# Gated differential attention on one core: the gate moved between the halves of a head's projection, and two kinds of DMA moved to other queues

## The chip, the cores and the metric

The kernel runs on 1 core of a Trainium2 chip. A core has TensorE (PE, matrix products into PSUM), VectorE (DVE), ScalarE (ACT), GpSimd (POOL) and SyncE (SP, which here only issues DMAs). DMAs are issued from the queues of SyncE, ScalarE or GpSimd and carried out beside the engines. The metric is the device time of one execution in microseconds (us): the median over runs, beside one profiled execution.

## The reference, cut to what matters

One layer of gated differential attention over 1024 tokens of width 1024, with 16 heads:

```python
h = rms_norm(x, norm_g)
q, k, v, z = jnp.split(h @ w_in, 4, axis=-1)          # each 1024 x 2048
q = rms_norm(q.reshape(b, s, 16, 2, 64), q_norm_g) * 64 ** -0.5
k = rms_norm(k.reshape(b, s, 16, 2, 64), k_norm_g)
v = v.reshape(b, s, 16, 128)
# causal, in blocks of 128 queries, with an ALiBi bias:
probs = softmax(einsum('bqhmd,bkhmd->bhmqk', qb, kb) + bias)
weights = probs[:, :, 0] - lam * probs[:, :, 1]
o = einsum('bhqk,bkhe->bqhe', weights, vb)
o = rms_norm(o, head_norm_g) * (1.0 - lam_0)
return x + (o.reshape(b, s, 2048) * jax.nn.silu(z)) @ w_out
```

## The kernel before

**Precision.** A float32 product is made of three float16 products (high by high, high by low, low by high), so each projection piece has three matmul lines: L370 to L372 for q, k, v and L447 to L449 for the gate z. `split_w` turns the raw weights of a head (`raww`, one buffer) into the high and low parts `wsp`: four `Square` passes for a scale (L160), a small matmul, four scalings (L199), and the low parts on VectorE (L205) or GpSimd (L202, L203).

**Heads and rounds.** Heads run in the order `heads`: the odd ones, then the even ones. In a round, `merge` interleaves two generators in proportion to their estimated costs: `attend` of the previous head (eight steps of scores, softmax and transposes, step i on (i+1)*128 keys, and the products with the values) and `project` of the present head. `project` of a head computes q, k and v in two halves of 512 tokens, `for c in range(2)`. A half has four pieces of 128 tokens, each in one PSUM tile `pg`. Each is read out by two ScalarE copies (L422, L423) and one VectorE instruction (L424). `norm(c)` then normalizes q and k of the half, transposes them by DMA (L393) and copies k (L396). After both halves come the two gates, one per 512 tokens: `gate(st, wt, 3, c)` accumulates 24 matmuls in one PSUM tile `pz` and reads it out by a chain that alternates ScalarE and VectorE: Exp (L452), min (L453), Ln (L454), max (L455), Exp (L456), product (L457). The last three heads (`LATE`: 10, 12, 14) project no gate; their three gates follow in `late_gates`.

**PSUM.** `pg`, `pz` and the output tiles share the three banks of the pool `ps_g`. The matmuls of a tile can't start before the tile that had the bank has been read out to its end: for a `pg` that is L424, for a `pz` it is L457.

**Buffers and queues.** The gate's result `sz` has 3 buffers. `finalize` multiplies the head's output with it on GpSimd (L537) and stores the product to DRAM (`g_dram`, L538); a buffer is free when its store has landed. SyncE's queue carries, in the order in which the scheduler put them, the loads of the next head's weights (L136, eight of 256 KB), the transposes of the weights p (L589) and of q and k (L393), the copies of k, and these stores. `prepare` takes one step of the next head's `split_w`; it is called at the end of each q, k, v piece and at every second step of a gate.

**What sets the order.** Each engine runs its instructions in one fixed order. The framework's scheduler sets it when the program is built, from the order of the code, buffers and its own estimates. DMAs of SyncE and ScalarE share eight completion semaphores (`DMAHW0` to `DMAHW7`), so a DMA also waits for the one that used its semaphore before.

## Time and profile before

| | us |
|---|---|
| median of 3 runs (1173.62 to 1181.43) | 1176.65 |
| the profiled execution | 1173.53 |
| its span, first to last instruction | 1171.8 |
| TensorE busy | 1109.9 |
| VectorE busy | 883.0 |
| ScalarE busy | 774.2 |
| GpSimd busy | 272.2 |

The profile's page lists busy time by engine, busy shares in 40 slices, the chain of work that ended last, and groups of instructions by line. Other views of the same trace list instructions in order of time, waits, and busy time by stretch. A matmul's busy time overlaps with its neighbours', so what TensorE could gain is read from its idle time and from start to start. In a row, "L370 PE MATMUL pg<-wsp,h" is line 370, an instruction that writes tile pg from wsp and h; "[2.27 <-DVE sz L457]" means that the engine sat idle for 2.27 us until VectorE's L457 had ended.

### The profile page before, as it was taken

The numbers are of one execution on the slowest core, as the hardware profiler recorded it, in microseconds if no ns is written. First come the engines' busy times: TensorE is split into PE (matmuls) and PEld (weight loads), VectorE is DVE, ScalarE is ACT, GpSimd is POOL, SyncE is SP. The second block draws the span as 40 slices with busy tenths as digits, with TensorE's granted clock in tenths as the row PEclk, the third lists the DMA queues.
The fourth block names the chain that finished last, engine by engine and source line by source line (L and its number), as shares of the span: only waits on it lengthen the run. The fifth ranks groups of instructions, "written<-read, shape, count | busy, mean of one in ns | idle before, by whom it ended". The sixth has DMA issues, their size and how long they took to land.

```text
span 1171.8 us, 18439 instructions
## 1 busy us (share of the span) xinstructions
PE 1109.9 (95%) x6154; PEld 668.5 (57%) x6154; DVE 883.0 (75%) x2180; ACT 774.2 (66%) x1713; POOL 272.2 (23%) x208
## 2 busy tenths in 40 slices
PE   4999999999999999999999999999899997999998
PEld 3555554545555555555545455555455534788887
DVE  6867869787978797879787878788888898563121
ACT  4757778787878797869686978787778776230000
POOL 2220314141314131314131313312121302031000
PEclk7999999999999999999999999999999988999999
DMA  7453736464646464646463645464564457685342
GB/s 222 109 119 52 164 67 140 89 140 85 139 90 137 88 143 89 146 80 133 93 144 76 140 93 126 93 129 100 105 137 87 109 125 182 143 292 179 112 130 70
DMA packets 327887, 143.50 MB, mean 122 GB/s; under 512 B 225136, under 2 KB 307312, under 8 KB 327792
## 3 DMA queue, kind: packets, MB, share of 16 engines
q1 hardware_dynamic: 323040, 133.93, 50.9%
q10 hardware_dynamic: 4752, 8.39, 2.7%
q8 instruction: 48, 0.79, 0.3%
q14 instruction: 47, 0.39, 0.1%
HBM read 63.11 MB, written 16.25 MB: 68 GB/s over the span
## 4 chain that ended last, share of the span: by engine, by line
PE 51%; DVE 20%; ACT 10%; issue 8%; DMA 6%; POOL 2%; SPq 2%; DVEq 0%; ACTq 0%; POOLq 0%
PE pg L370 8%; PE pg L371 8%; PE pg L372 8%; DVE p L559 6%; PE pf L498 5%; PE pf L499 5%; PE pf L500 5%; PE pss L570 3%; DMA raww<-in_l_w_in_dram 3%; DVE p L584 2%; ACT p L576 2%; ACT wsp L160 2%; ACT wsp L199 2%; DMA wt<-p 2%; PE po L601 2%
## 5 line engine op out<-in xcount | busy, mean ns | idle before, releaser
L370 PE MATMUL pg<-wsp,h 128*128 128x384 f16 x1024 | 336.3, 328 | 21.0 <-DVE sz L457 11.9
L372 PE MATMUL pg<-wsp,h 128*128 128x384 f16 x1024 | 336.4, 329 | 1.1 <-DVE h L278 1.1
L371 PE MATMUL pg<-wsp,h 128*128 128x384 f16 x1024 | 336.3, 328 | 1.2 <-POOL wsp L203 1.2
L576 ACT ACTIVATE p<-p,mn 128x128 f32<-128x128 f32 (+7 forms) x256 | 196.4, 768 | 61.0 <-DVE mn L559 59.8
L559 DVE CUSTOM_DVE_ANT_0 p<-pss,toep,nsl 128x512 f32<-128x512 f32 (+3 forms) x256 | 161.2, 642 | 36.8 <-DMA wt<-p 24.6
L570 PE MATMUL pss<-qk 128*128 128x512 f16 (+3 forms) x768 | 164.6, 327 | 11.6 <-DVE mn L559 11.5
L371 PEld LDWEIGHTS <-h 128*128 128x128 f16 x1024 | 100.7, 98 | 86.7 <-issue 26.5
L372 PEld LDWEIGHTS <-h 128*128 128x128 f16 x1024 | 100.6, 98 | 68.2 <-issue 3.7
L66 ACT ACTIVATE p<-p,rc 128x128 f16<-128x128 f32 (+7 forms) x128 | 98.6, 771 | 61.8 <-DVE p L584 60.7
L370 PEld LDWEIGHTS <-h 128*128 128x128 f16 x1024 | 100.7, 98 | 66.6 <-issue 4.1
L584 DVE SCALAR_TENSOR_TENSOR p<-p,rc,p 128x128 f32<-128x128 f32 (+7 forms) x128 | 116.9, 914 | 1.5
L587 DVE SCALAR_TENSOR_TENSOR p<-p,rc,p 128x128 f16<-128x128 f32 (+7 forms) x128 | 104.7, 820 | 14.8 <-ACT p L66 14.6
L570 PEld LDWEIGHTS <-qk 128*128 128x128 f16 x768 | 71.0, 98 | 72.2 <-issue 18.6
L447 PE MATMUL pz<-h,wsp 128*128 128x512 f16 x256 | 98.3, 384 | 1.3 <-DVE sz L457 1.3
L448 PE MATMUL pz<-h,wsp 128*128 128x512 f16 x256 | 98.3, 384 | 0.0
L614 POOL TENSOR_TENSOR sql<-sqo,sqh 128x512 fp32r<-128x512 f32 x30 | 41.7, 1390 | 243.3 <-ACT sqh L612 243.3
L449 PE MATMUL pz<-h,wsp 128*128 128x512 f16 x256 | 98.1, 383 | 0.0
L537 POOL TENSOR_TENSOR sz<-sqo,sz 128x512 f32<-128x512 f32 x26 | 37.7, 1448 | 184.4 <-DVE sqo L631 150.0
L202 POOL TENSOR_SCALAR raww<-raww,scw 128x1024 f32<-128x1024 f32 (+1 forms) x31 | 42.3, 1371 | 159.1 <-ACT wsp L199 127.9
L559 DVE CUSTOM_DVE_ANT_0 p<-pss,toep,mn 128x128 f32<-128x128 f32 (+3 forms) x128 | 75.6, 601 | 0.0
L160 ACT ACTIVATE wsp<-raww 128x1024 f16<-128x1024 f32 x61 | 63.6, 1044 | 14.7 <-DMA raww<-in_l_w_in_dram 9.4
L503 DVE TENSOR_TENSOR xr<-pf,xr 128x512 f32<-128x512 f32 (+1 forms) x33 | 22.1, 671 | 63.4 <-PE pf L500 62.5
(160 smaller groups left out, 2082.9 us busy)
## 6 DMA issues: line engine op xcount, KB each, us to landing
raww<-in_l_w_in_dram SPq DMA_DIRECT2D x96, 256.0 KB, 3.8
rawo<-in_l_w_out_dram SPq DMA_DIRECT2D x32, 256.0 KB, 4.5
qk<-qk SPq DMA_DIRECT2D x64, 128.0 KB, 2.4
raww<-in_l_w_in_dram SPq DMA_DIRECT2D x40, 192.0 KB, 3.7
g_dram<-sz SPq DMA_DIRECT2D x30, 256.0 KB, 2.3
rawg<-g_dram ACTq DMA_DIRECT2D x24, 256.0 KB, 3.5
xt<-in_x_dram SPq DMA_DIRECT2D x8, 512.0 KB, 5.3
xr<-in_x_dram SPq DMA_DIRECT2D x16, 256.0 KB, 3.5
```

Of the source, the lines that this page charges most:

```text
L66: A.activation(out, in_, AF.Copy, scale=scale)
L370: T.matmul(pg, a_h, w_h, start=k == 0, stop=False)
L371: T.matmul(pg, a_h, w_l, start=False, stop=False)
L372: T.matmul(pg, a_l, w_h, start=False, stop=k == KT - 1)
L447: T.matmul(pz, wt["hi"][:, k, n], hh[c][:, k], start=k == 0, stop=False)
L448: T.matmul(pz, wt["hi"][:, k, n], hl[c][:, k], start=False, stop=False)
L449: T.matmul(pz, wt["lo"][:, k, n], hh[c][:, k], start=False, stop=k == KT - 1)
L559: V.tensor_tensor_reduce(out=pm[m][:, o:o + w], in0=pss[:, :w], in1=toep[:, u:u + w], scale=nslope, scalar=3e38 if prev[m] is None else pr ...
L570: T.matmul(pss[m][:, :w].rearrange("p (t q) -> p t q", q=P), qk[:, c, 0, i % 4, m], qk[:, b, v, :w // P, m], start=v == 1, stop=v == 2)
L576: A.activation(pm[m][:, :n], pm[m][:, :n], AF.Exp, scale=-1.0, bias=prev[m], accum_out=sx[:, 1 - m:2 - m])
L584: V.scalar_tensor_tensor(out=p0, in0=p1, scalar=rc[:, 0:1], in1=p0, op0=ALU.mult, op1=ALU.add)
L587: V.scalar_tensor_tensor(out=pl[:, n:], in0=p0, scalar=rc[:, 1:2], in1=pl[:, :n], op0=ALU.mult, op1=ALU.subtract)
```

## The change

The gates of a head are projected between its two halves of q, k, v instead of after them, except in the first head, which keeps its order. `prepare` is called after every half piece in the first half, at every second gate step as before, and at the end of each piece in the second half. The loads of `w_in` are issued from ScalarE's queue, except the first head's; those of a head are put behind the reading of the first piece of the second half (`marks`) of the head two before it. The stores of gated heads are issued from GpSimd's queue. `sz` gets a fourth buffer, and the tile `sqo` of the attention shares the two buffers of `sqk` instead of having its own. Lines behind L136 are numbered 2 to 10 higher in the changed kernel.

```diff
--- before.py
+++ after.py
@@ -133,7 +133,7 @@
             for k in range(KT):
                 rows = wq_view[k * P:(k + 1) * P]
                 bs = slice(blocks[0], blocks[-1] + 1)
-                ins = Q.dma_start(raw[:, k, bs], rows[:, 3, hd] if isinstance(hd, slice) else rows[:, bs, hd])
+                ins = (Q if hd == heads[0] else A).dma_start(raw[:, k, bs], rows[:, 3, hd] if isinstance(hd, slice) else rows[:, bs, hd])
                 if hd == heads[0]:
                     tc.keep_in_program_order(ins)
             return raw, blocks
@@ -351,6 +351,8 @@
         tmp = pool(main, "tmp", bufs=1, reuse_waits="tile")
         sm = pool(main, "sm", bufs=3, reuse_waits="tile")
 
+        marks = []
+
         def project(hd, wt, st):
 
             qk = qkp.tile([P, 2, 3, 4, 2, P], F16, name="qk", tag="qk")
@@ -400,7 +402,10 @@
                 prep.append(split_w(raw0, range(3, 4), wt, hd))
             if nx is not None:
                 st["wt"] = {}
-                prep.append(split_w(*load_raw(nx), st["wt"], nx))
+
+                with tc.issue_after(marks[-1].ins) if marks else ExitStack():
+                    loaded = load_raw(nx)
+                prep.append(split_w(*loaded, st["wt"], nx))
 
             def prepare(pb):
 
@@ -411,7 +416,7 @@
                         return
                     prep.pop(0)
 
-            for c in range(2):
+            def qkv(c):
                 rw = tmp.tile([P, 2, 4, P], F32, name="rw", tag="rw", bufs=2)
                 for t in range(4):
                     pb = ps_g.tile([P, 512], F32, name="pg", tag="pg")
@@ -419,24 +424,29 @@
                     for hf in range(2):
                         gemm_piece(pg, c, t * P, range(hf * 4, hf * 4 + 4))
                         if hf:
-                            A.activation(rw[:, :, t], pg[:, :256].rearrange("p (s b) -> p s b", s=2), AF.Copy)
+                            ev = A.activation(rw[:, :, t], pg[:, :256].rearrange("p (s b) -> p s b", s=2), AF.Copy)
                             A.activation(vh[:, c * 4 + t], pg[:, 256:], AF.Copy, scale=vsc)
                             V.scalar_tensor_tensor(out=vl[:, c * 4 + t], in0=pg[:, 256:], scalar=vsc,
                                                    in1=vh[:, c * 4 + t], op0=ALU.mult, op1=ALU.subtract)
-                            prepare(lambda: pb[:, 384:])
-                        elif hd == heads[0]:
+                            if c or hd != heads[0] or len(prep) > 1:
+                                prepare(lambda: pb[:, 384:])
+                            if t == 0 and c == 1:
+                                marks.append(ev)
+                        elif c == 0 and hd != heads[0] or hd == heads[0] and len(prep) > 1:
                             prepare(None)
                         yield 2.1
                 norm(c, rw)
-            if hd in LATE:
-                while prep:
-                    prepare(None)
-                return
-            for c in range(2):
-                for k in gate(st, wt, 3, c):
-                    if k % 2:
-                        prepare(None)
-                    yield 0.69
+            yield from qkv(0)
+            if hd == heads[0]:
+                yield from qkv(1)
+            if hd not in LATE:
+                for c in range(2):
+                    for k in gate(st, wt, 3, c):
+                        if k % 2:
+                            prepare(None)
+                        yield 0.69
+            if hd != heads[0]:
+                yield from qkv(1)
             while prep:
                 prepare(None)
 
@@ -448,7 +458,7 @@
                 T.matmul(pz, wt["hi"][:, k, n], hl[c][:, k], start=False, stop=False)
                 T.matmul(pz, wt["lo"][:, k, n], hh[c][:, k], start=False, stop=k == KT - 1)
                 yield k
-            e = vp.tile([P, 512], F32, name="sz", tag="sz", bufs=3)
+            e = vp.tile([P, 512], F32, name="sz", tag="sz", bufs=4)
             A.activation(e, pz, AF.Exp, scale=wt["inv"][:, 1, n:n + 1])
             V.tensor_scalar(e, e, 1e18, None, ALU.min)
             A.activation(e, e, AF.Ln, bias=1.0)
@@ -535,7 +545,7 @@
                 return
             e = V if hd in LATE else G
             e.tensor_tensor(z, t1, z, ALU.mult)
-            Q.dma_start(g_dram[c][:, :, place[hd], :].rearrange("t p e -> p t e"), z.rearrange("p (t e) -> p t e", t=4))
+            G.dma_start(g_dram[c][:, :, place[hd], :].rearrange("t p e -> p t e"), z.rearrange("p (t e) -> p t e", t=4))
 
         def attend(hd, st):
 
@@ -605,7 +615,7 @@
                         yield 6 * (4 - il) * P / 2400
                 os = tmp.tile([P, 512], F32, name="os", tag="os")
                 A.activation(os, po, AF.Copy, scale=st["unit"])
-                sq = tmp.tile([P, 512], F32, name="sqo", tag="sqo")
+                sq = tmp.tile([P, 1024], F32, name="sqo", tag="sqk", bufs=2)[:, :512]
                 A.activation(sq, os, AF.Square)
                 sqh = tmp.tile([P, 512], F32R, name="sqh", tag="sqh")
                 e = V if hd == heads[-1] else G
```

On TensorE, before: the end of the fourth head's second gate (`pz_2854`) and the start of the fifth head's first q, k, v piece (`pg_2926`); the score matmuls (`pss`) between them are those of the attention.

```order
L570 LDWEIGHTS qk_2246
L570 MATMUL pss_2902<-qk_2246 128x128
L370 LDWEIGHTS h0_83
L370 MATMUL pg_2926<-wsp_2311,h0_83 128x384
L371 LDWEIGHTS h0_83
L371 MATMUL pg_2926<-wsp_2311,h0_83 128x384
```

In the change the fourth head's second gate (`pz_2585`) is followed by a piece of the same head's second half (`pg_2663`, tokens from `h1`):

```order
L459 LDWEIGHTS wsp_1609
L459 MATMUL pz_2585<-h1_84,wsp_1609 128x512
L372 LDWEIGHTS h1_84
L372 MATMUL pg_2663<-wsp_1609,h1_84 128x384
L373 LDWEIGHTS h1_84
L373 MATMUL pg_2663<-wsp_1609,h1_84 128x384
```

So a gate's bank is now asked for by the second half of its own head, and before by the next head.

On ScalarE, before: from the next head's `Square` passes (L160) to the Exp of the fifth head's second gate (L452, the last row). The names behind "waits" are semaphores: `DMAHW` of DMAs, `Pool`, `DVE` and `PE` of engines.

```order
L160 ACTIVATE wsp,bd<-raww 128x8x128 [waits DMAHW3_49,DMAHW4_49,DMAHW2_49,DMAHW5_49,DMAHW1_49,DMAHW6_49,DMAHW0_49,PE_49]
L391 ACTIVATE sqk<-rw 128x16x64 [waits DVE_49]
L160 ACTIVATE wsp,bd<-raww 128x8x128 x3
L576 ACTIVATE p_3563,sums_458<-p_3563,mn 128x128 [waits DVE_49]
L66 ACTIVATE p_3487<-p_3486,rc 128x1024 [waits DVE_49]
L576 ACTIVATE p_3564,sums_458<-p_3564,mn 128x128 [waits DMAHW7_49,DVE_49]
L422 ACTIVATE rw<-pg 128x2x128 [waits PE_49]
L423 ACTIVATE vh<-pg 128x128
L576 ACTIVATE p_3614,sums_459<-p_3614,mn 128x256 [waits DVE_49,Activation_49]
L576 ACTIVATE p_3615,sums_459<-p_3615,mn 128x256 [waits DMAHW1_49,DVE_49]
L578 ACTIVATE sums_458<-sums_458,nlam 128x1 [waits Activation_49]
L452 ACTIVATE sz<-pz,inv 128x512 [waits DMAHW2_49,Pool_49]
```

In the change, the same gate's Exp is L462; `L136 DMA` are the loads, L617 to L622 read out a product with the values, and L586 and L66 belong to the softmax.

```order
L136 DMA raww<-in_l_w_in_dram 128x4x128
L393 ACTIVATE sqk<-rw 128x16x64 [waits DVE_49]
L617 ACTIVATE os<-po,un 128x512 [waits PE_49]
L136 DMA raww<-in_l_w_in_dram 128x4x128 [waits DMAHW2_49]
L136 DMA raww<-in_l_w_in_dram 128x4x128 [waits DMAHW3_49]
L136 DMA raww<-in_l_w_in_dram 128x4x128
L66 ACTIVATE p_3287<-p_3286,rc 128x768 [waits DVE_49,Activation_49]
L619 ACTIVATE sqo<-os 128x512 [waits Activation_49,Pool_49]
L622 ACTIVATE sqh<-os 128x512
L136 DMA raww<-in_l_w_in_dram 128x4x128 [waits DMAHW5_49]
L462 ACTIVATE sz<-pz,inv 128x512 [waits DMASW5_49]
L136 DMA raww<-in_l_w_in_dram 128x4x128 [waits DMAHW6_49]
```

The Exp stood behind the next head's `Square` passes and the reading of its first piece (L422); it now stands among the loads of the next head's weights, ahead of these passes, and waits for a DMA of GpSimd's queue (`DMASW`).

On SyncE, before, one head's stretch: transposes of p and q/k, loads, a store.

```order
L589 DMA_TRANSPOSE wt_6568<-p_6567 128x10x128
L136 DMA raww<-in_l_w_in_dram 128x4x128 x4
L589 DMA_TRANSPOSE wt_6568<-p_6616 128x12x128
L136 DMA raww<-in_l_w_in_dram 128x4x128 x4
L589 DMA_TRANSPOSE wt_6568<-p_6727 128x14x128
L393 DMA_TRANSPOSE qk<-sqk 128x16x128
L538 DMA g_dram_61<-sz 128x4x128
L396 DMA qk<-qk 64x1024 x2
L589 DMA_TRANSPOSE wt_6568<-p_6813 128x16x128
```

In the change, and below it GpSimd's queue over one head and a bit, with the stores (L548):

```order
L599 DMA_TRANSPOSE wt_5887<-p_5886 128x10x128
L395 DMA_TRANSPOSE qk<-sqk 128x16x128
L599 DMA_TRANSPOSE wt_5887<-p_5947 128x12x128
L398 DMA qk<-qk 64x1024 x2
L599 DMA_TRANSPOSE wt_5887<-p_6061 128x14x128
L599 DMA_TRANSPOSE wt_5887<-p_6129 128x16x128
L599 DMA_TRANSPOSE wt_6226<-p_6225 128x2x128
L599 DMA_TRANSPOSE wt_6226<-p_6280 128x4x128
```

```order
L202 TENSOR_SCALAR raww<-raww,scw 128x8x128 x2
L203 TENSOR_TENSOR wsp<-raww,wsp 128x8x128 x2
L624 TENSOR_TENSOR sql<-sqo,sqh 128x512
L387 TENSOR_TENSOR rw<-rw,gain 128x512
L547 TENSOR_TENSOR sz<-sqo,sz 128x512
L548 DMA g_dram_62<-sz 128x4x128
L624 TENSOR_TENSOR sql<-sqo,sqh 128x512
L547 TENSOR_TENSOR sz<-sqo,sz 128x512
L548 DMA g_dram_61<-sz 128x4x128
```

SyncE keeps the transposes and the copies of k; a store stands directly behind the product (L547) that it stores.

## Rows read from the trace of the kernel before

**Rows 1.** Page, part 1: busy us, share of the span, instructions of each engine.
```profile
PE 1109.9 (95%) x6154; PEld 668.5 (57%) x6154; DVE 883.0 (75%) x2180; ACT 774.2 (66%) x1713; POOL 272.2 (23%) x208
```

**Rows 2.** Busy us by stretch: length, PE, PEld, DVE, ACT, POOL, PEclk, DMA, GB/s.
```profile
22.30:79.80 57.50, 52.71 (x302) 32.28 (x302) 44.23 (x125) 37.88 (x86) 21.34 (x15) 0.92 0.42 114
...
135.20:191.40 56.20, 56.20 (x333) 31.60 (x330) 44.85 (x118) 41.21 (x97) 16.07 (x11) 1.00 0.52 121
...
250.70:309.40 58.70, 56.43 (x333) 31.65 (x331) 48.32 (x122) 46.59 (x105) 15.99 (x10) 1.00 0.55 114
...
871.90:1005.00 133.10, 118.29 (x598) 64.93 (x597) 116.60 (x274) 98.77 (x209) 25.26 (x20) 0.95 0.58 132
```

**Rows 3.** What TensorE waited for, 60 to 820 us: total us, times, longest.
```profile
PE pg L370 <- DVE sz L457: 11.9, 8, 2.3
PE pg L370 <- DVE vl L424: 5.1, 5, 1.6
PE pss L570 <- DVE mn L559: 2.2, 3, 1.4
```

**Rows 4.** TensorE in order of time (start, us, [wait]) up to 258.12 us.
```profile
230.85 0.38 PE L601 MATMUL po<-wt,vh 128*128 128x512 f16 x1
231.06 0.38 PE L602 MATMUL po<-wt,vl 128*128 128x512 f16 x1
...
243.72 0.38 PE L449 MATMUL pz<-h,wsp 128*128 128x512 f16 x1
...
250.25 0.38 PE L449 MATMUL pz<-h,wsp 128*128 128x512 f16 x1
...
250.69 0.33 PE L370 MATMUL pg<-wsp,h 128*128 128x384 f16 x1
...
255.03 0.81 PE L570 MATMUL pss<-qk 128*128 128x384 f16 x4
258.12 0.32 PE L370 MATMUL pg<-wsp,h 128*128 128x384 f16 x1 [2.27 <-DVE sz L457]
```

**Rows 5.** ScalarE in order of time, same stretch: either gate's first Exp.
```profile
246.47 0.67 ACT L452 ACTIVATE sz<-pz,inv 128x512 f32<-128x512 f32 x1
...
264.06 0.69 ACT L452 ACTIVATE sz<-pz,inv 128x512 f32<-128x512 f32 x1 [1.20 <-DMA g_dram<-sz]
```

**Rows 6.** VectorE in order of time: the last step of either gate.
```profile
257.32 0.74 DVE L457 SCALAR_TENSOR_TENSOR sz<-pz,inv,sz 128x512 f32<-128x512 f32 x1
...
269.43 0.74 DVE L457 SCALAR_TENSOR_TENSOR sz<-pz,inv,sz 128x512 f32<-128x512 f32 x1
```

**Rows 7.** DMA issues on SyncE and ScalarE by line: duration ns min/median/max.
```profile
L136 SPq DMA_DIRECT2D raww<-in_l_w_in_dram x144: 327/621/2015, 1.2 to 875.1; - x144
L484 ACTq DMA_DIRECT2D rawg<-g_dram x32: 326/326/477, 904.8 to 1142.3; - x32
L538 SPq DMA_DIRECT2D g_dram<-sz x30: 364/383/1147, 122.1 to 991.9; - x30
```

**Rows 8.** SyncE in order of time: loads between two transposes.
```profile
358.41 2.62 SPq L136 DMA_DIRECT2D raww<-in_l_w_in_dram  x4
362.48 1.45 SPq L589 DMA_TRANSPOSE wt<-p  x1
```

**Rows 9.** What ScalarE waited for up to 820 us: the gate buffer.
```profile
ACT sz L452 <- DMA g_dram<-sz: 2.6, 3, 1.2
```

**Rows 10.** GpSimd's TENSOR_TENSOR of one size: duration ns min/median/max.
```profile
L614 POOL TENSOR_TENSOR sql<-sqo,sqh x30: 1267/1274/1998, 111.2 to 976.9; 128x512 fp32r<-128x512 f32 x30
```

**Rows 11.** SyncE in order of time: the loads for the second and third head.
```profile
41.60 5.40 SPq L136 DMA_DIRECT2D raww<-in_l_w_in_dram  x8
...
73.43 6.93 SPq L136 DMA_DIRECT2D raww<-in_l_w_in_dram  x8
```

**Rows 12.** Busy time by stretch around a fall of the granted clock (PEclk).
```profile
600.00:620.00 20.00, 17.88 (x102) 10.17 (x101) 15.70 (x40) 18.06 (x47) 2.19 (x1) 0.91 0.71 147
```

**Rows 13.** What TensorE waited for from 820 to 1000 us.
```profile
PE pss L570 <- DVE mn L559: 9.2, 9, 2.5
```

## What the change does to the time

> **What bounds the kernel now.** I read the page's busy shares first. TensorE is busy 1109.9 us of 1171.8, VectorE 883.0, ScalarE 774.2, GpSimd 272.2 [rows 1]: nothing but TensorE is near its limit over the whole. Then the busy time by stretch, one stretch for each head [rows 2]. The reader is to see three kinds of stretch there. In the round from 135.2 us TensorE is busy 56.20 of 56.20: that is the floor of a round. A usual round, from 250.7, has 56.43 busy of 58.70, so 2.3 us idle, while VectorE (48.3) and ScalarE (46.6) have some 10 us to spare. In the last rounds, 871.9 to 1005, VectorE has 116.6 of 133.1, and TensorE waits for it. The output after 1005 isn't touched.
>
> Next, what TensorE waited for between 60 and 820 us [rows 3]. Two rows make nearly all of it, both at a `pg` (L370) that wants a PSUM bank: 11.9 us for the gate's product L457 and 5.1 us for L424, the reading of an earlier `pg`. Together they are 17.0 us, plus 2.2 us of scores that wait for the maximum (L559).
>
> The views in order of time show how one arises. The first gate's last matmul ends at 243.72 + 0.38 = 244.10, the second's at 250.63; then comes a piece of the next head, and the following piece could start at 255.03 + 0.81 = 255.84 but starts at 258.12, after 2.27 us for L457 [rows 4]. So TensorE has 255.84 - 244.10 = 11.7 us of other work before it wants the first gate's bank again. The chain that frees it runs from 244.10 over the Exp at 246.47 [rows 5] to the product's end at 257.32 + 0.74 = 258.06 [rows 6]: 14.0 us. The second gate's chain is longer still: its Exp starts only at 264.06 and its product ends at 270.17, 19.5 us after its matmuls. Its bank is out for so long that the next pieces rotate on two banks, which is the L424 row.
>
> **The change part by part.** *Gates between the halves.* No work is added; 24 matmuls of a gate are the same wherever they stand. What counts is TensorE's work between a gate and the next use of its bank. In the changed order 24 gate matmuls, a piece, six instead of four score matmuls of 512 columns, and twelve of an attention output (three each of 512, 384, 256 and 128 columns) stand there; four score matmuls of 384 columns are gone. A matmul of 512 columns starts 231.06 - 230.85 = 0.21 us after the one before it [rows 4]. By columns that is +0.42 for the scores, -0.63 for those gone and 3 x 1280 / 512 x 0.21 = +1.6 for the output: 11.7 becomes 13.1 us. The gates also stand in the attention's middle steps, on 512 to 768 keys and not on 896 and 1024, so the softmax work that its chain queues behind is shorter; my estimate is a chain of 9 to 12 us in place of 14.0. Both move the right way, so I take most of the 11.9 us away. The second gate is another matter: its Exp (now L462) still stands late in ScalarE's order, behind the reading of a piece, an output and six loads. Its bank stays out, and pieces still rotate on two banks. By the same count of columns the time that TensorE gives them rises from about 5 to 6 to 7 us, so I take some of the 5.1 us away too. Together 14 of the 17.0 us; of the 2.2 us for the maximum 1 us, since SyncE brings the transposed weights sooner (next part). That is **-15**. Bounds: -5 if only the first gate's wait halves, -21 if all 19.2 us go and with them the last idle time.
>
> *Loads on ScalarE's queue.* Eight of them a head leave SyncE, where one takes 0.327 to 2.015 us to issue, median 0.621 [rows 7], and where four stand as a block of 2.62 us ahead of a transpose [rows 8]. On ScalarE the nearest row is its own issue of other loads, 0.326 to 0.477 us [rows 7]. So 8 x 0.33 to 8 x 0.62 = 2.6 to 5.0 us a head, and ScalarE has 46.6 of 58.7 us filled [rows 2]: hidden over the round. If that cover were gone it would be 2.6 to 5 us for each of some 12 heads. What is queued behind a load is what stands there in the order: readings of pieces, softmax, the gate's Exp. For the wait on semaphores I take nothing, as the transfers named are old by then.
>
> At the start it isn't hidden. There, the loads of the third head stand on ScalarE in one block ahead of the readings of the second head's pieces, and wait for GpSimd to free `raww`. SyncE took 5.40 and 6.93 us for eight of them there [rows 11]; at ScalarE's 0.326 it would be 2.6. TensorE can lose nothing (if it has pieces left to do) up to 8 us (a block of 6.93 and a reading). I take **+2**, near ScalarE's own row.
>
> *Stores on GpSimd's queue.* SyncE gives away an issue of 0.383 us [rows 7], twice a head. No row shows a DMA of GpSimd. From below it costs nothing: GpSimd is busy 23% [rows 1], and with a fourth `sz` buffer a store has a gate more of time, so that the 2.6 us which ScalarE waited for stores [rows 9] should go. From above: 26 stores at SyncE's 0.383 are +10 if each comes on the path. GpSimd's own instructions are stretched at times, one of 1.267 us to 1.998 [rows 10]. I take **0**, because nothing waits behind the store on GpSimd for long.
>
> A rule of the Trainium skill speaks against this part. "SBUF — State Buffer", section "SBUF: two separate sides", says that a DMA from GpSimd's queue needs descriptors that GpSimd writes through a port shared with VectorE, and that VectorE can lock it out for as long as an instruction runs; it advises the other two queues. By it the stores land late, which is R2 below with its time. The stretch in [rows 10] fits a shared port, and no run here shows it for a store.
>
> *Late part and the clock.* From 871.9 on VectorE's 116.6 us of work is unchanged, and the scores wait for it, 9.2 us from 820 to 1000 [rows 13]. Sooner transposes could give up to -5 there, loads in bursts on ScalarE cost up to +6; I take **0**. A stretch at half clock is seen at 600 to 620, where the mean granted clock is 0.91 [rows 12]; it lies in a round with idle time. Whether it goes is in the bounds (1.6 us at most).
>
> *The sum* is -15 + 2 + 0 + 0 = -13. The profiled execution has 1173.5 us and becomes 1160.5; the median of the three runs is 3.1 above it, so for a median I say 1163.
>
> **The rivals.** *R1, the waits move to the second half.* Between the readings of its first and second piece ScalarE has about 6.9 us of work and eight loads, 9.5 to 11.8 us; TensorE has about 6 to 7 us of work before it wants a bank that is read there. If the reading of a piece is late by 3 us, and the rotation on two banks hides half, 1.5 us a head come back, 11 x 1.5 = 16 us. That takes the gain: 1173.5 - 13 + 16 = 1176, and 1166 to 1181 by how much is hidden. For it speaks that [rows 5] shows the Exp held by ScalarE's order and not by TensorE; against it that the softmax work there is shorter.
>
> *R2, slower: a store comes late.* The second gate's Exp waits for a store from GpSimd's queue, and behind it on ScalarE stand the readings of all further pieces. Before, this wait was 1.20 us once and 2.6 in all [rows 5, 9]. If GpSimd issues or lands a store so late that ScalarE stands 5 us or more at that Exp, TensorE has no more than 1.5 to 2 us left to hide it, and loses 3 us in each of 12 heads: -13 + 36 = +23, about 1197. It decides against the change from about 2 us of TensorE time a head (24 - 13 = +11). For it speaks that the store stands directly behind a product on GpSimd, which has splits of the weights ahead; against it the fourth buffer.
>
> *R3, nothing changes.* The second gate's Exp is as late as before and the first gate's gain is swallowed by the block of loads at the start and by the clock: -15 + 8 + 4 gives about 1171 to 1174.
>
> **How the numbers follow.** My forecast has 0.53, R1 0.22, R2 0.12, R3 0.13. The forecast's own range is 1152 (-21 and -3 late) to 1171 (-5 and +3). About 1% is what a measurement of this kernel can tell from no change: below 1164.9 or above 1188.4. Of the forecast 0.46 lies below 1164.9 and 0.07 above it; R1 and R3 lie within, and of R2 0.10 lies above 1188.4, with 0.02 of R1. So faster 0.46, same 0.42, slower 0.12. The range that leaves out 2 in 10 runs from 1150 to 1182.
>
> **What would show it.** Right: in the view of waits the row of L370's successor (L372) on the gate's product falls from 11.9 to under 3 us, that on the reading of a piece (L424, now L429) doesn't grow; a usual round takes 57 us. R1: the row on the reading grows by what the gate's row loses. R2: ScalarE shows a wait of several us at L462 for a DMA from `sz`, and TensorE's waits stand just behind it. The start is wrong if the second round loses more than 8 us. The stores: GpSimd's issue rows much over 0.8 us. What would make the prediction wrong as a whole is a longer span in rounds with less TensorE idle time, by the clock, which I can't see ahead of the run.

## The result: 1192.22 us, slower by 1.4%

The changed kernel takes 1192.22 us (median of 4 runs, 1190.80 to 1196.35), the kernel before beside it 1175.13. The ratio is 1.0142, 95% interval 1.0093 to 1.0192. 1163 was forecast, with 1150 to 1182 as the range over all rivals. The profiled execution has a span of 1189.0 us, 17.2 more than before's.

Page, part 1 of the changed kernel; [rows 1] is the same line before:

```profile
PE 1115.9 (94%) x6154; PEld 671.3 (56%) x6154; DVE 907.9 (76%) x2180; ACT 770.1 (65%) x1713; POOL 295.5 (25%) x238
```

TensorE is busy 6.0 us longer, though it does the same matmuls; the other 11.2 of the 17.2 us are idle time. Busy time by stretch tells where. First the changed kernel (length, PE, PEld, DVE, ACT, POOL, PEclk, DMA, GB/s, as in [rows 2]): the rounds of the first three heads, a usual one, the ten rounds of the fourth to thirteenth head, and all behind them:

```profile
22.60:84.40 61.80, 55.81 (x312) 33.24 (x312) 45.40 (x132) 37.23 (x86) 14.76 (x11) 0.90 0.34 91
84.40:146.60 62.20, 54.21 (x289) 29.20 (x289) 52.32 (x112) 42.71 (x95) 23.11 (x12) 0.92 0.44 92
146.60:217.30 70.70, 60.62 (x335) 32.75 (x333) 49.99 (x118) 45.02 (x99) 16.19 (x11) 0.95 0.57 108
275.80:334.30 58.50, 56.62 (x333) 31.58 (x331) 50.14 (x123) 45.37 (x103) 16.43 (x13) 1.00 0.55 113
217.30:801.40 584.10, 565.59 (x3295) 315.57 (x3293) 499.20 (x1220) 452.77 (x1018) 167.48 (x124) 1.00 0.57 112
801.40:1189.00 387.60, 370.75 (x1892) 252.18 (x1889) 247.89 (x559) 183.84 (x402) 73.05 (x72) 0.99 0.54 139
```

The kernel before in the stretches that [rows 2] doesn't have, its second round first:

```profile
79.80:135.20 55.40, 53.59 (x308) 29.87 (x306) 44.55 (x116) 41.34 (x93) 11.75 (x7) 0.97 0.50 89
191.40:776.70 585.30, 567.20 (x3293) 316.59 (x3291) 487.53 (x1226) 461.47 (x1022) 154.74 (x102) 1.00 0.55 113
776.70:1171.80 395.10, 372.87 (x1893) 251.52 (x1890) 248.71 (x558) 183.76 (x401) 67.35 (x64) 0.98 0.54 137
```

So the fourth head starts at 217.3 us in place of 191.4: **25.9 us are lost in the first three rounds.** The next ten rounds take 584.1 us in place of 585.3, and all behind them 387.6 in place of 395.1. 25.9 - 1.2 - 7.5 = 17.2. Round by round the first three take 4.3, 6.8 and 14.5 us more than before's. Of their loss 17.5 us are idle time (24.1 us idle in 194.7, before 6.6 in 169.1), and 8.1 us are longer busy time for nearly the same matmuls: the mean granted clock is 0.90, 0.92 and 0.95, before 0.92, 0.97 and 1.00.

What TensorE waited for in the ten rounds, then in the first three, in the changed kernel (us, times, longest):

```profile
PE po L611 <- DMA wt<-p: 8.4, 8, 2.1
PE pss L580 <- DMA qk<-qk: 6.9, 6, 2.5
PE po L611 <- issue: 3.2, 4, 0.9
```

```profile
PE pmn L631 <- POOL sql L624: 4.7, 1, 4.7
PE pg L373 <- POOL wsp L203: 4.5, 2, 3.2
...
PE pss L580 <- DVE mn L569: 3.1, 2, 1.9
...
PE po L611 <- DMA wt<-p: 3.0, 1, 3.0
PE po L611 <- ACT sz L462: 2.9, 1, 2.9
```

The two rows of [rows 3] that the forecast spoke of, 11.9 and 5.1 us, are gone, as forecast. In their place stand 8.4 us for the transposed weights, 6.9 us for the copies of k and 3.2 us of issue (waits of the same matmuls L611 for which the profile shows no releaser), 18.5 together, none of which the prediction had.

**The wait for the copies of k, step by step.** The changed kernel in the fourth head's round, in order of time: loads on ScalarE's queue, VectorE's L394 (the last step of the first half's norm), SyncE's transpose of that half's q and k, its copies, and the first scores of the same head on TensorE.

```profile
257.73 0.55 ACTq L136 DMA_DIRECT2D raww<-in_l_w_in_dram  x1
...
260.82 1.99 ACTq L136 DMA_DIRECT2D raww<-in_l_w_in_dram  x2
...
262.89 1.22 DVE L394 TENSOR_TENSOR sqk<-rw,sqk 128x1024 f16<-128x1024 f32 x1
...
264.14 4.51 SPq L395 DMA_TRANSPOSE qk<-sqk  x1
...
272.73 1.10 SPq L398 DMA_DIRECT2D qk<-qk  x2
...
275.63 0.34 PE L580 MATMUL pss<-qk 128*128 128x128 f16 x3 [0.97 <-DMA qk<-qk]
```

The same chain in the kernel before, in the fifth head's round:

```profile
283.58 1.22 DVE L392 TENSOR_TENSOR sqk<-rw,sqk 128x1024 f16<-128x1024 f32 x1
...
284.86 1.73 SPq L393 DMA_TRANSPOSE qk<-sqk  x1
289.16 1.11 SPq L396 DMA_DIRECT2D qk<-qk  x2
...
309.15 0.39 PE L570 MATMUL pss<-qk 128*128 128x128 f16 x4
```

Before, the norm's last step L392 ended at 284.80, the copies were issued at 289.16, 4.3 us after the transpose, and the scores came 20 us later. In the changed kernel the copies can be issued only at 272.73, 8.6 us after the transpose, and the scores wait 0.97 us. The first half's pieces had ended at 237.8 (before 275.3), so the norm's end is 26 us behind them in place of 9.5. In VectorE's order it is the 45th instruction behind the last reading of the first half, before the 13th.

**The wait for the transposed weights.** It comes once in nearly every round, at the first matmul of the values of the first half (L611), some 40 us in. The same rounds, SyncE's transposes of p and that matmul, in the changed kernel and then before:

```profile
252.96 4.26 SPq L599 DMA_TRANSPOSE wt<-p  x3
...
257.81 0.38 PE L611 MATMUL po<-wt,vh 128*128 128x512 f16 x1 [0.91 <-DMA wt<-p]
```

```profile
263.37 12.68 SPq L589 DMA_TRANSPOSE wt<-p  x5
...
289.52 0.38 PE L601 MATMUL po<-wt,vh 128*128 128x512 f16 x1
```

The matmul needs the weights of the attention's fourth step. Their transpose is the second of the three, issued at 254.4 and landed at 257.7, just when TensorE wants it. Before, it is the last of the five, issued at 274.8 and landed at 278.7, 10.8 us ahead of its use. It takes 3.3 us now and 4.0 before, so it isn't slower; it is issued 13 us later in the round (37.1 us in, before 24.1). In the ten rounds it is issued 36 to 38 us in, before 22 to 26. The softmax that makes these weights now stands behind splits (L205) and among the first gate's chain in VectorE's order. The experiments below tell the parts of the change apart here. With the new calls of `prepare` alone (h2_before_halfprep) it is issued 20 to 24 us in, with the queues alone (e7_queues) 25 to 31. With the gates moved and without those calls (i1_prep_before) it is 30 to 38, and 27 to 32 with the loads back on SyncE too (h4_prep_before_sp). So the calls don't delay it; the gates' new place and the loads' queue do.

### The profile page after: what moved, and what is told of

The parts are those of the page before. It is cut to its first block, busy times and chain, and to the rows that moved or that the text cites. A ratio compares the mean times of both kernels' runs of the same rounds, so it can differ in the third digit from the quotient of the medians.

```text
span 1189.0 us, 18391 instructions
## 1 busy us (share of the span) xinstructions
PE 1115.9 (94%) x6154; PEld 671.3 (56%) x6154; DVE 907.9 (76%) x2180; ACT 770.1 (65%) x1713; POOL 295.5 (25%) x238
## 4 chain that ended last, share of the span: by engine, by line
PE 55%; DVE 16%; DMA 14%; ACT 7%; issue 5%; POOL 2%; ACTq 1%; SPq 0%; DVEq 0%; POOLq 0%
PE pg L374 8%; PE pg L373 8%; PE pg L372 8%; DMA qk<-sqk 5%; PE pss L580 5%; PE pf L508 4%; PE pf L510 4%; PE pf L509 4%; DMA wt<-p 3%; DVE p L569 3%; PE pz L457 3%; PE pz L458 3%; PE pz L459 3%; DVE p L594 2%; PE po L611 2%
## 5 line engine op out<-in xcount | busy, mean ns | idle before, releaser
L586 ACT ACTIVATE p<-p,mn 128x128 f32<-128x128 f32 (+7 forms) x256 | 196.2, 769 | 50.0 <-DVE mn L569 47.7
L66 ACT ACTIVATE p<-p,rc 128x128 f16<-128x128 f32 (+7 forms) x128 | 98.9, 773 | 45.7 <-DVE p L594 45.3
L597 DVE SCALAR_TENSOR_TENSOR p<-p,rc,p 128x128 f16<-128x128 f32 (+7 forms) x128 | 124.5, 974 | 4.6 <-ACT p L66 4.5
L202 POOL TENSOR_SCALAR raww<-raww,scw 128x1024 f32<-128x1024 f32 (+1 forms) x31 | 49.8, 1612 | 220.5 <-ACT wsp L199 92.1
L547 POOL TENSOR_TENSOR sz<-sqo,sz 128x512 f32<-128x512 f32 x26 | 35.7, 1372 | 204.1 <-DVE sqo L641 114.7
L611 PE MATMUL po<-wt,vh 128*128 128x512 f16 x192 | 63.4, 330 | 18.3 <-DMA wt<-p 11.4
L199 ACT ACTIVATE wsp<-raww,scw 128x1024 f16<-128x1024 f32 (+1 forms) x67 | 69.0, 1098 | 7.3 <-DVE scw L180 7.2
L160 ACT ACTIVATE wsp<-raww 128x1024 f16<-128x1024 f32 x61 | 63.7, 1052 | 8.6 <-DMA qk<-qk 4.0
```

The lines of the kernel that those rows point to most:

```text
L66: A.activation(out, in_, AF.Copy, scale=scale)
L586: A.activation(pm[m][:, :n], pm[m][:, :n], AF.Exp, scale=-1.0, bias=prev[m], accum_out=sx[:, 1 - m:2 - m])
L597: V.scalar_tensor_tensor(out=pl[:, n:], in0=p0, scalar=rc[:, 1:2], in1=pl[:, :n], op0=ALU.mult, op1=ALU.subtract)
```

## The experiments

The medians below stand beside runs of the kernel before on the same chip. "Start" is the time up to the fourth head's first piece, "ten rounds" and "rest" are the two stretches above; "loads" is where in a usual round the eight loads are issued (us from its first piece). The three stretches are those of one profiled execution each. Kernels with the same order in a stretch differ by 2 us in the start (before, j1, j2, f6), 3 in the ten rounds (the change, e3, e4, e5: 583.3 to 586.3) and 5 in the rest (the change, e3, e4, e5, f3, f6: 387.6 to 392.4). So the ten rounds' 1.2 us are no gain that can be told from none.

| kernel | us | ratio, interval | start | ten rounds | rest | loads |
|---|---|---|---|---|---|---|
| before | 1175.1 | | 191.4 | 585.3 | 395.1 | SyncE, 49 to 59 |
| the change | 1192.2 | 1.014 (1.009 to 1.019) | 217.3 | 584.1 | 387.6 | ScalarE, 40 to 48 |
| e1_gates | 1257.2 | 1.071 (1.068 to 1.074) | 223.0 | 632.4 | 394.9 | SyncE, 34 to 51 |
| e7_queues | 1239.3 | 1.056 (1.055 to 1.058) | 194.1 | 644.4 | 398.6 | ScalarE, 55 to 63 |
| e4_first3_sp | 1205.3 | 1.028 (1.025 to 1.031) | 225.4 | 583.3 | 392.4 | ScalarE, 40 to 48 |
| e5_head0_rule | 1195.5 | 1.018 (1.016 to 1.021) | 217.3 | 585.6 | 392.2 | ScalarE, 40 to 48 |
| f3_old3 | 1192.9 | 1.015 (1.011 to 1.019) | 197.8 | 604.8 | 391.7 | ScalarE, 40 to 48 |
| f6_old3_sp4 | 1190.6 | 1.014 (1.010 to 1.018) | 192.4 | 609.4 | 389.2 | ScalarE, 40 to 48 |
| f5_no_marks | 1217.5 | 1.036 (1.032 to 1.040) | 217.3 | 604.8 | 394.8 | ScalarE, 30 to 46 |
| e2_loads_sp | 1203.3 | 1.025 (1.022 to 1.028) | 220.5 | 591.8 | 388.8 | SyncE, 31 to 43 |
| i1_prep_before | 1283.2 | 1.094 (1.090 to 1.098) | 209.5 | 674.7 | 399.3 | ScalarE, 9 to 16 |
| h2_before_halfprep | 1178.1 | 1.004 (1.002 to 1.006) | 201.9 | 583.5 | 389.3 | SyncE, 33 to 41 |
| h4_prep_before_sp | 1236.2 | 1.055 (1.051 to 1.058) | 195.3 | 635.0 | 400.4 | SyncE, 7 to 16 |
| g1_mark_t2 | 1312.1 | 1.118 (1.113 to 1.123) | 212.4 | 700.7 | 399.7 | ScalarE, 61 to 72 |
| e3_stores_sp | 1193.3 | 1.017 (1.014 to 1.019) | 213.9 | 586.3 | 391.3 | ScalarE, 40 to 48 |
| f2_old3_halfprep | 1193.6 | 1.017 (1.014 to 1.020) | 211.7 | 590.7 | 390.8 | ScalarE, 40 to 51 |
| j1_late_halfprep | 1169.1 | 0.997 (0.995 to 0.998) | 190.9 | 585.3 | 390.7 | SyncE, 49 to 59 |
| j2_late_halfprep_sz4 | 1175.5 | 1.002 (1.000 to 1.004) | 192.6 | 591.0 | 391.2 | SyncE, 49 to 59 |

**The gates alone (e1_gates), the queues alone (e7_queues).** In e1_gates the gates and the new calls of `prepare` stay, everything else is as before; in e7_queues the reverse.

```diff
 # e1_gates, against the changed kernel
-ins = (Q if hd == heads[0] else A).dma_start(
+ins = Q.dma_start(
-with tc.issue_after(marks[-1].ins) if marks else ExitStack():
+with ExitStack():
-G.dma_start(g_dram[c]        # sz with 3 buffers, sqo a tile of its own
+Q.dma_start(g_dram[c]
 # e7_queues, against the kernel before
-ins = Q.dma_start(
+ins = (Q if hd == heads[0] else A).dma_start(
-Q.dma_start(g_dram[c]        # sz with 4 buffers, sqo in sqk's
+G.dma_start(g_dram[c]
```

> Only the gates stand between the halves, with the changed kernel's calls of prepare; loads and stores stay on SyncE's queue, sz keeps 3 buffers and sqo its own. Theory T1 (the first three rounds lose their 26 us to the eight loads that stand as a block on ScalarE, 5.93 us at 93.6, and to what the late weights push back): without that block the two waits of the kernel before are gone and nothing takes their place, ratio to before 0.985 to 0.992, about 1160 us. Theory T2 (the gate's place and the calls of prepare themselves push the splitting of the next head's weights into GpSimd's and ScalarE's way in the first rounds, whatever queue loads them): ratio 1.005 to 1.015, about 1187 us.

> The kernel before with the loads of later heads on ScalarE's queue, the stores of gated heads on GpSimd's, sz with 4 buffers and sqo in sqk's; the gates stay behind both halves and prepare is called as before. T1: the loss comes with the loads, ratio 1.008 to 1.02, 1185 to 1198 us, with the idle time in the first three rounds. T2: the loss doesn't come, ratio 0.995 to 1.003, 1170 to 1179 us, and TensorE's waits for L457 and L424 stay at about 17 us.

Neither theory had this: each half alone is four to five times as bad as both. T1 falls as the whole cause with e1_gates (no load on ScalarE, and the start loses 32 us); for e7_queues the start is nearly right and it is the usual rounds that lose, 64.4 us in place of 58.5. One of them, TensorE, VectorE and the queues of ScalarE and SyncE:

```profile
380.92 1.23 ACTq L136 DMA_DIRECT2D raww<-in_l_w_in_dram  x2
...
384.26 1.33 ACTq L136 DMA_DIRECT2D raww<-in_l_w_in_dram  x2
...
384.58 12.32 SPq L589 DMA_TRANSPOSE wt<-p  x2
...
385.64 0.69 ACT L623 ACTIVATE sqo<-pmn,eps_t 128x512 f32<-128x512 f32 x1 [1.28 <-issue]
...
393.25 0.35 DVE L559 CUSTOM_DVE_ANT_0 p<-pss,toep,nsl 128x128 f32<-128x128 f32 x1 [3.06 <-DMA wt<-p]
...
398.07 0.72 PE L570 MATMUL pss<-qk 128*128 128x512 f16 x2 [3.92 <-DVE mn L559]
```

The loads are issued from 378.9 to 385.6, among the softmax of the longest rows; ScalarE waits for its own issue (1.28 us). A transpose of p that SyncE issues at 384.58 has landed only at 393.1, 8.5 us later. It is the sixth step's. In the ten rounds that step's transposes take 8.6 us at the median here and 4.3 before, though loads are in flight beside all of them in both kernels; before, the loads are on SyncE's own queue. VectorE wants that p's buffer and waits 3.06 us, and the scores behind it wait 3.92 us for VectorE. So the waits here come from a transpose that lands late beside ScalarE's loads, more than from the 5 us of issue.

**The first three heads' loads on SyncE (e4_first3_sp); the condition in the first head taken out (e5_head0_rule).**

```diff
 # e4_first3_sp
-ins = (Q if hd == heads[0] else A).dma_start(
+ins = (Q if hd in heads[:3] else A).dma_start(
 # e5_head0_rule
-if c or hd != heads[0] or len(prep) > 1:
-    prepare(lambda: pb[:, 384:])
+prepare(lambda: pb[:, 384:])
-elif c == 0 and hd != heads[0] or hd == heads[0] and len(prep) > 1:
+elif c == 0 and hd != heads[0] or hd == heads[0]:
```

> The changed kernel, but the loads of the first three heads in SyncE's queue; the others stay on ScalarE's. T1: the block ahead of the readings at 93 us is gone, the first three rounds lose about 20 us in place of 45, ratio to before 0.99 to 1.0, 1163 to 1175 us. T2: they still lose 38 to 45 us, ratio 1.008 to 1.015.

> The changed kernel, but prepare is called after each half piece of the first head without the condition on the length of its list, so that the second head's weights are split sooner. T1: no effect or a few us, ratio to before 1.010 to 1.016. T2, if the condition in the first head is what delays the second head's weights: the waits for L199 and L203 at 56 and 60 us go, with the clock's fall behind them, ratio 0.998 to 1.007.

The block of loads on ScalarE was real: in the changed kernel seven of them end the idle time of a reading.

```profile
93.58 5.93 ACTq L136 DMA_DIRECT2D raww<-in_l_w_in_dram  x7
99.55 0.38 ACT L427 ACTIVATE rw<-pg 128x256 f32<-128x256 f32 x1 [5.35 <-DMA raww<-in_l_w_in_dram]
```

Without it (e4_first3_sp) the start is 8 us longer still, but that doesn't price the block, since another wait comes in: in e4's second round the first half's norm ends only at 139.6 and TensorE waits for its transposed q and k.

```profile
145.60 0.82 PE L580 MATMUL pss<-qk 128*128 128x128 f16 x4 [11.24 <-DMA qk<-sqk]
```

Less these 11.2 us (an estimate by subtraction), e4's start would be only some 3 us shorter than the changed kernel's, so the block isn't what costs 25.9. What it does cost shows in the next two kernels. The condition in the first head isn't the cause either.

**The first three heads in the old order (f3_old3), with loads on SyncE up to the fourth (f6_old3_sp4).**

```diff
-if hd == heads[0]:
+if hd in heads[:3]:
     yield from qkv(1)
-if hd != heads[0]:
+if hd not in heads[:3]:
     yield from qkv(1)
 # prepare as in the kernel before in these heads; f6_old3_sp4 also:
-ins = (Q if hd == heads[0] else A).dma_start(
+ins = (Q if hd in heads[:4] else A).dma_start(
```

> The changed kernel, but the first three heads (not only the first) keep the gates behind both halves, with prepare called in them as in the kernel before. Theory S (the changed kernel is slower by its first three rounds, where 45 us of TensorE's time are lost in place of 19, because the second head's and third head's rounds in the new order put norms, transposes and the splitting of weights in each other's way): the first three rounds lose 20 to 26 us, the later ones stay at 2 to 4 us each, ratio to before 0.992 to 1.000, about 1170 us. Theory Q (the loss at the start follows the queues, wherever the gates are): the first three rounds still lose 38 us or more, ratio 1.008 or more.

> As the kernel before it, and the loads of the first four heads on SyncE's queue. Theory S: no difference to it beyond 5 us, since the block of loads on ScalarE was not what cost the time. Theory Q: this one recovers the 20 us at the start and the other does not.

The start is nearly before's (197.8 and 192.4), but the total stays. The 5.4 us between the two starts are the price of these loads on ScalarE, most of it in the second round: 58.8 us in f3, 53.9 in f6. In f3 ScalarE's loads go out from 76.6 to 84.1 and the split waits for them, and behind it the reading of a piece:

```profile
91.33 1.06 ACT L160 ACTIVATE wsp<-raww 128x1024 f16<-128x1024 f32 x1 [5.98 <-DMA raww<-in_l_w_in_dram]
...
98.88 0.48 PE L372 MATMUL pg<-wsp,h 128*128 128x384 f16 x1 [5.29 <-DVE vl L429]
```

Third and fourth round of f3_old3:

```profile
141.60:197.80 56.20, 56.20 (x332) 31.62 (x330) 45.79 (x118) 41.20 (x96) 17.41 (x12) 1.00 0.49 113
197.80:269.50 71.70, 59.23 (x334) 32.28 (x332) 54.70 (x129) 52.20 (x114) 17.81 (x13) 0.93 0.64 115
```

The third round is the floor, 56.2 us; the fourth, the first with the new order, takes 71.7 at a clock of 0.93. **The loss moves with the change of order:** put off by two heads, it comes in the fourth round. In the changed kernel, where the order changes in the second round, the third loses most. Theory S had the place right and the saving wrong.

**Is it the gates' place or the calls of prepare? (h2_before_halfprep, i1_prep_before, f2_old3_halfprep.)** The first is the kernel before with the calls after the half pieces; the second the changed kernel without them; the third has the calls from the second head on, and the gates moved from the fourth.

```diff
 # h2_before_halfprep, against the kernel before
-elif hd == heads[0]:
+elif c == 0 or hd == heads[0]:
     prepare(None)
 # i1_prep_before, against the changed kernel: e5_head0_rule's first edit, and
-elif c == 0 and hd != heads[0] or hd == heads[0] and len(prep) > 1:
+elif hd == heads[0]:
     prepare(None)
 # f2_old3_halfprep: the two edits of qkv(1) in f3_old3, without those of prepare
```

> The kernel before with one thing of the change alone: prepare is also called after the first half of each piece in the first half of every head. Theory N: the norm of the first half comes later here too, but behind it the second half and both gates still stand ahead of the next head's scores, so the later rounds lose little (0 to 2 us each) and the first rounds some: ratio 1.000 to 1.015. Rival G: nothing moves, ratio 0.997 to 1.003.

> The changed kernel with prepare called as in the kernel before: at the end of each piece and at every second gate step, not after each half piece of the first half. Theory N (the calls after half pieces crowd the whole split of the next head's weights into the first half's pieces, so that on VectorE and ScalarE it stands ahead of the norm of that half: its last step L394 comes 24 us after the pieces in place of 8, the copies of k land when the next head's first scores are due, and the first rounds lose most by it): that step comes 8 to 12 us after the pieces again, TensorE's wait for the copies of k (6.9 us) goes, and the first three rounds lose 20 to 30 us in place of 45; ratio to before 0.985 to 1.000. Rival G (the gates' own chains ahead of the norm delay it, whenever the split runs): no change, ratio 1.008 to 1.016.

> The changed kernel with the gates behind both halves in the first three heads, but with prepare called after the half pieces from the second head on. So the split moves forward in the round first (as in the kernel before with these calls, which lost 10 us in the third round), and the gates move three rounds later. Theory A (the two moves cost their own: gates about 17 us, calls about 10 us, wherever each takes place): the third or second round loses 8 to 12 us more than before's, the fourth and fifth 12 to 18 us more, ratio 1.010 to 1.020. Rival B (the gates' move costs only because the split has to move in the same rounds): with the split already early the fourth and fifth rounds lose at most 6 us more, ratio 1.000 to 1.008.

The third round of h2_before_halfprep, and the third and fourth of f2_old3_halfprep:

```profile
136.40:201.90 65.50, 59.69 (x333) 32.71 (x332) 47.12 (x122) 43.00 (x99) 14.70 (x9) 0.95 0.49 107
```

```profile
139.70:211.70 72.00, 60.55 (x334) 32.67 (x332) 53.78 (x126) 47.80 (x108) 18.22 (x13) 0.95 0.59 118
211.70:271.90 60.20, 56.96 (x333) 31.74 (x331) 49.06 (x123) 47.57 (x104) 17.67 (x13) 1.00 0.59 114
```

With the calls alone the third round takes 65.5 us in place of 56.2, with the changed kernel's queues and buffers too 72.0. When the gates then move (211.7 on) the round takes 60.2, some 2 us more than usual: by the rounds that is rival B, not A, though the ratio of 1.017 lies in A's range, since the third round lost more than either had. On GpSimd the split of the next head's weights stands 43 to 45 us into a round before and 23 us in the changed kernel: it moves forward by a third of a round, within one or two rounds, and norms, transposes and splits meet there. In the changed kernel's second round GpSimd shows one such meeting:

```profile
126.83 5.12 POOL L202 TENSOR_SCALAR raww<-raww,scw 128x1024 f32<-128x1024 f32 x2 [10.81 <-DVE wsp L205]
131.92 2.29 POOL L203 TENSOR_TENSOR wsp<-raww,wsp 128x1024 f16<-128x1024 f32 x1
134.17 2.11 POOL L624 TENSOR_TENSOR sql<-sqo,sqh 128x512 fp32r<-128x512 f32 x1
...
136.33 0.80 PE L631 MATMUL pmn<-sql,ones 128*128 128x512 f32 x1 [4.68 <-POOL sql L624]
```

Its two L202 take 5.12 us (a pair takes 2.21 at 84.5), and `sql` stands behind one L203; TensorE waits 4.68 us for it.

i1_prep_before says what the calls are for. Theory N's mechanism is there: the scores of the next head have 14 us to spare again behind the copies of k, and that wait is gone. The rest of its forecast failed. The start still takes 209.5 us, 18.1 more than before's, though the split is no longer early, so the calls aren't all that costs there. And the split now ends at the turn of the round, the loads come 9 us into the next, and each round takes 67.5 us:

```profile
357.95 4.00 ACTq L136 DMA_DIRECT2D raww<-in_l_w_in_dram  x4
...
358.21 5.05 SPq L598 DMA_TRANSPOSE wt<-p  x1
...
361.99 1.06 ACT L393 ACTIVATE sqk<-rw 128x1024 f16<-128x1024 f32 x1 [3.85 <-DMA raww<-in_l_w_in_dram]
...
370.08 0.58 PE L610 MATMUL po<-wt,vh 128*128 128x512 f16 x1 [3.06 <-DMA wt<-p]
...
370.17 0.62 DVE L568 CUSTOM_DVE_ANT_0 p<-pss,toep,nsl 128x384 f32<-128x384 f32 x1 [9.34 <-DMA wt<-p]
```

The eighth step's transpose, issued at 358.21 with eight loads in flight, lands at 370.0, 11.8 us later (10.5 at the median of the ten rounds; before, with no loads beside it, 4.4). VectorE waits 9.34 us and TensorE 3.06 for it.

**Where the loads stand (f5_no_marks, e2_loads_sp, g1_mark_t2, h4_prep_before_sp).**

```diff
 # f5_no_marks
-with tc.issue_after(marks[-1].ins) if marks else ExitStack():
+with ExitStack():
 # e2_loads_sp, and h4_prep_before_sp on top of i1_prep_before
-ins = (Q if hd == heads[0] else A).dma_start(
+ins = Q.dma_start(
 # g1_mark_t2
-if t == 0 and c == 1:
+if t == 2 and c == 1:
     marks.append(ev)
```

> The changed kernel without the tie of a head's loads to the reading of a piece two heads before, so that they may stand earlier in ScalarE's order. Theory M (gates alone and queues alone both lost 6 to 10 us in every later round because loads were free to stand early, as a block ahead of readings or transposes, and the tie is what keeps the changed kernel's later rounds as short as before's): later rounds of 61 to 66 us in place of 58.5, ratio to before 1.04 to 1.07. Rival: the tie does nothing, ratio 1.010 to 1.018, and the two parts need each other for another reason.

> The changed kernel with all loads on SyncE's queue again, still tied to the reading of a piece. Theory M: with the tie the queue matters little, later rounds stay at 57 to 60 us, ratio 1.010 to 1.025. Rival (the gates' new place can't stand loads between SyncE's transposes, whenever they come): rounds of 62 to 67 us as with the gates alone, ratio 1.05 to 1.07.

> The changed kernel with a head's loads tied to the third piece of the second half in place of the first, about 10 us later. Theory D (the loads, in flight together with the first half's transposes of q and k, double these from 4.3 to 8.5 us, and that alone eats the last of the 16 us that the next head's scores had): the transposes land after 4 to 5 us again and the wait for the copies of k goes, each later round is about 1 us shorter, ratio 1.002 to 1.010. Theory N: the transposes get shorter, but the norm is still 24 us late, and the first rounds lose what they lost: ratio 1.008 to 1.018.

> As the first kernel of this set, with all loads on SyncE's queue (still tied to the reading of a piece). Theory N: with the split spread out the queue of the loads decides little, within 8 us of that kernel; loads on SyncE stand ahead of transposes there, so not faster than it. Rival: the loads on ScalarE's queue are what costs, and this one is faster by more than 8 us.

Theory M holds for the tie in the main: without it ten rounds take 604.8 us (60.5 a round, 61 to 66 forecast), with it on SyncE 591.8. Theory D had the mechanism right and the outcome wrong: tied two pieces later, the loads leave the transposes of q and k alone (4.4 us at the median) and the wait for the copies of k is gone, but they fall from 61 us to the end of the round, as in e7_queues, and the rounds grow to 70 us, with 44.9 us of waits for transposed weights. Over the table (leaving out the kernels whose order changes within the ten rounds), loads on ScalarE at 40 to 48 us give ten rounds of 583 to 586 us; at 30 to 46 they give 605, at the end of the round 644 to 701 and at its beginning 675. That the loads' place sets the time of a round is shown by f5_no_marks and g1_mark_t2, which change nothing else. That transposes which land late are a part of the way is shown by h4_prep_before_sp, where the loads stand at the same place as in i1_prep_before, but on SyncE's queue: loads are in flight beside the eighth step's transposes in all ten rounds again, but these land after 4.8 us in place of 10.5, and the ten rounds take 635.0 us in place of 674.7. That is the rival's outcome, and theory N's forecast of at most 8 us between the two missed. The rest of h4's loss, and e1_gates's, has another cause: the transposes of p land in the usual time there (3.6 us at the median of all steps, as before), TensorE waits mostly for VectorE, and what holds VectorE was not followed.

**Stores on SyncE again (e3_stores_sp).**

```diff
-G.dma_start(g_dram[c]
+Q.dma_start(g_dram[c]
```

> The changed kernel with the stores of gated heads in SyncE's queue again. If the stores on GpSimd cost nothing (the prediction's term): ratio to the kernel before 1.008 to 1.022, with the same 45 us in the first three rounds. Rival (a late store holds the second gate's Exp, as 3.4 us once in the third round): the first three rounds lose 5 us less and the wait of ScalarE for the store of sz is gone, ratio 1.005 to 1.010.

1193.3 us beside 1192.2: the stores' queue makes no difference in the total that can be seen. In one place it does: in the changed kernel's third round ScalarE waits 3.4 us at L462 for a store, and TensorE 2.9 us behind it; in e3 ScalarE's wait is 0.8 us, TensorE's is gone, and the round takes 67.2 us in place of 70.7. The later stretches are 2 and 4 us longer, as much as such kernels differ anyway. An issue on GpSimd takes about twice SyncE's 0.383 us [rows 7]:

```profile
L548 POOL DMA_DIRECT2D g_dram<-sz x30: 755/802/957, 145.0 to 1008.3; - x30
```

**What can be had from it (j1_late_halfprep, j2_late_halfprep_sz4).** The rest after the ten rounds is 7.5 us shorter in the change (2.7 to 5.9 in e3, e4, e5, f3 and f6), and 5.8 in h2_before_halfprep. So only the last three heads get the calls:

```diff
-elif hd == heads[0]:
+elif hd == heads[0] or c == 0 and hd in LATE:
     prepare(None)
 # j2_late_halfprep_sz4 also: sz with 4 buffers, sqo in sqk's
```

> The kernel before with one part of the change in its last three heads only (those without gates): prepare also after the first half of each piece in the first half. These rounds lost 5 to 8 us less in the changed kernel and in the kernel before with the calls everywhere. Theory L (the calls give that by themselves, without the cost in the first rounds): ratio 0.993 to 0.997, about 1168 us. Rival: the gain needs the earlier rounds' early split too, ratio 0.998 to 1.002.

> As the kernel before it, with four buffers of sz and sqo in sqk's buffers. The second gate's Exp no longer waits for a store (2.6 us of ScalarE's waits in the kernel before). If that wait cost TensorE anything through the bank: 1 to 4 us less than that kernel. If it was hidden: no difference to it.

j1_late_halfprep takes 1169.1 us, ratio 0.9967 (0.9953 to 0.9981), a little faster than both kernels. The round from 820.2 us takes 47.5 us; before, the one from 820.4 took 51.5 (first row before, second row j1_late_halfprep):

```profile
820.40:871.90 51.50, 47.28 (x283) 26.82 (x282) 43.72 (x114) 38.81 (x92) 11.92 (x8) 1.00 0.54 103
```

```profile
820.20:867.70 47.50, 46.27 (x283) 26.85 (x282) 44.39 (x115) 38.13 (x90) 12.43 (x8) 1.00 0.61 122
```

Why it helps there is not separated; these heads have no gates for the split to fall into, so it ended late without the calls. j2_late_halfprep_sz4 takes that gain away again, 6.4 us at the median, which neither expectation had. ScalarE's wait for a store is gone (2.3 us in j1's ten rounds), but TensorE waits 20.0 us for the gate's product there, before 11.5. Whether the fourth buffer does it or the sharing of `sqk`'s buffers was not separated.

## Why the prediction was wrong, step by step

1192.22 us lies above the forecast's range and above the 1188.4 from which the prediction itself counts a result as slower, to which it gave 0.12. Its sum holds, but the ends of its range, 1152 and 1171, stand on two bases, the median and the profiled execution, both without the +2; from the median and with it they are 1155 and 1177.

- **"-15" for the gates between the halves.** The wait that it named did go: the first gate's chain takes 11.2 us (PE's last matmul at 362.3, product's end at 373.5; forecast 9 to 12), both waits of [rows 3] are zero. But the ten rounds gain 1.2 us, since as much came back. The failing sentence is "No work is added; 24 matmuls of a gate are the same wherever they stand. What counts is TensorE's work between a gate and the next use of its bank." It counted one consumer. The first half's norm, its transpose and the copies of k had 20 us to spare before, as the rows above show; the change puts the split and the gates' chains ahead of them, and TensorE then waits 6.9 us for k. Without the new calls 14 us are spare again (i1_prep_before), so the early split takes most of the 20; the gates' part is read from VectorE's order. The other 8.4 us contradict the sentence that took 1 us off "since SyncE brings the transposed weights sooner": the fourth step's come 13 us later in the round and lose the 10.8 us that they had to spare. The waits went from VectorE's to SyncE's rows.
- **"+2" at the start.** 25.9 were measured. The prediction saw only the eight loads on ScalarE there, and for these alone its 0 to +8 fits: f3_old3 against f6_old3_sp4 gives 5.4 us. It passed over the calls of `prepare`, which the diff shows, as work that moves at no cost; alone they cost the start 10.5 us (h2_before_halfprep). The new place of the gates was priced only for the later rounds; without the calls the start still loses 18.1 us (i1_prep_before). The parts don't add up to 25.9, since each also moves the others.
- **Loads "hidden over the round", 2.6 to 5.0 us a head.** The issue takes 0.547 us at the median, 4.4 us a head, and is hidden in the changed kernel. That it is hidden only at that place in the round, e7_queues, i1_prep_before and g1_mark_t2 show. The price when it isn't was forecast as 2.6 to 5 us a head; these kernels lose 6 to 12 us a round. Transposes that land late are a part of it: 4 us a round between i1_prep_before and h4_prep_before_sp.
- **Stores: 0.** Right for the total (e3_stores_sp). A rule of the Trainium skill that the prediction weighed ("SBUF — State Buffer", section "SBUF: two separate sides") would have had them late; the trace shows one wait of 3.4 us at L462 for a store, in the third round, which TensorE pays with 2.9 us, and none later.
- **Late part: 0, bounds -5 to +6.** -7.5 was measured, beyond the bound, but -2.7 to -5.9 in the five other kernels with the same late part. The calls give most of it (-5.8 in h2_before_halfprep, -4.4 in j1_late_halfprep), not the sooner transposes that the bound was made of.
- **Rivals.** R1 had the gain taken away by waits for readings in the second half; the gain was taken away, but by transposes and copies. R2 had the right sign; its cause, a late store, shows once and costs 2.9 us. R3's "swallowed by the start and the clock" is nearest, at a chance of 0.13; 8 us for the start was a third of what came, and the clock's part there (8.1 us) was taken as 4.

What stays open: which of the meetings in the first rounds costs how much (the waits there are nine rows of 1 to 5 us, and the clock is lower beside them), how the delay of the fourth step's weights divides between gates and loads, and whether a slower advance of the split would help.

## What to carry to other kernels

When a piece of work moves in front of another, list the consumers of everything that is now behind it, DMA chains too, and how long each of them had to spare; here the wait removed cost TensorE some 2 us a round, while the norm that lost its slack had had 20 and the transposed weights 11. Parts of a change that move work in time (loads, splits, calls) are tried at the place where they land in the round, since each alone can be far worse than all together. And a change of order had a price here in the rounds in which it took effect; look at the first rounds apart from the steady ones.

## What the runs showed of the hardware

- DMA transposes on SyncE's queue landed late beside loads of 256 KB on ScalarE's queue, and hardly beside loads on SyncE's own. Medians of the ten rounds, loads in flight beside every one: the sixth step's 8.6 us with ScalarE's loads (e7_queues) and 4.3 with SyncE's (before); the eighth step's 10.5 (i1_prep_before) and 4.8 (h4_prep_before_sp), and 4.4 with none in flight (before). A page of the Trainium skill ("Trainium Kernel Development and Optimization", section "Key Constraints") says that the queues of SyncE, ScalarE and GpSimd run on the same 16 DMA engines and interleave, so that issuing from several saves only issue time. These figures agree that the queues share, but not with the "only": here the queue of the loads also decided when the transposes landed.
- A store issued by GpSimd takes 0.755 to 0.957 us there and lands after 3.8 us at the median; SyncE's landed after 2.3.
- In the first three rounds 17.5 us more of idle time came with 8.1 us more of busy time, at mean granted clocks of 0.90, 0.92 and 0.95 in place of 0.92, 0.97 and 1.00.
